# Pair 0 of an attention layer: the units of two heads issued in turns of two

## The chip, the cores and the metric

The kernel runs on one core of a Trainium2 chip. A core has a matrix engine (TensorE, PE in the profile, with its weight loads listed as PEld), three engines for elementwise work (VectorE or DVE, ScalarE or ACT, GpSimd or POOL), and a SyncE (SP) whose queue issues most DMA transfers. Each engine runs its own stream of instructions and waits for the others by semaphores. The metric is the device time of one execution in microseconds (us); the median of a few runs is given.

## The reference

The layer has 1024 positions and a width of 1024. The input is normalised and modulated, projected, mixed by 16 heads of 64, gated, projected again, added to the input and normalised. Eight heads do forgetting attention (a softmax). The other eight, with which the kernel begins, do stick-breaking attention:

```python
z = jnp.einsum('bhqd,bhkd->bhqk', q, k).astype(jnp.float32) * scale
strict = k_pos[None, :] < q_pos[:, None]
log_beta = jax.nn.log_sigmoid(z)
log_keep = jnp.where(strict, jax.nn.log_sigmoid(-z), 0.0)
later = lax.cumsum(log_keep, axis=3, reverse=True) - log_keep
w = jnp.where(strict, jnp.exp(log_beta + later), 0.0)
return jnp.einsum('bhqk,bhkd->bhqd', w.astype(v.dtype), v)
```

A query block of 128 rows sees only the keys up to its own end, so block i works on (i+1) x 128 keys.

## The kernel before

**Precision.** A matrix product in full precision is made of three (or two, with packed operands) products of fp32r parts: every operand is split into a rounded part ("hi") and the rest ("lo").

**Stages.** After a start phase (inputs, modulation, normalisation and transposition of x, and the projections of the first two pairs) comes the attention stage, from about 91 us on. The 16 heads form 8 pairs; pairs 0 to 3 are stick-breaking, pairs 4 to 7 forgetting attention. A *unit* (p, h, i) is query block i of head h of pair p; there are 16 to a pair, 128 in all.

**What a unit does** (stick-breaking):
- `att_query` (L383): ACT copies the unit's queries into one of two small buffers of its head (L388).
- `att_scores` (L397): PE writes the scores into the tile S (L410, L411). S has one buffer, two PSUM banks wide. ACT reads it twice, for the sigmoid of -z (L430, tile kp) and of z (L431, tile be). DVE makes the reverse running product of kp in one scan (L436), or two where there are more than 512 keys (L440), and POOL multiplies be by it (L444).
- `att_transpose` (L448): PE transposes the result 128 x 128 at a time into tiles T of up to four blocks (L461; two buffers). ACT casts each tile to its hi part (L463), DVE makes the lo part (L464), both called pt.
- `att_pv` (L469): once two neighbouring blocks 2j and 2j+1 of a head are transposed, PE multiplies them with v (L476), with 4j + 4 products, hi parts first. Block kb of v is needed by the product of key block kb; the last key block, 2j+1, comes after the first 2j hi products (or after one, for j = 0). ACT and DVE add up the result (L495, L496), POOL gates it (L497) and SP stores it (L505).

**Fillers.** Between these PE works on projections for later pairs, cut into steps by generators (`fillers`, L923). For pair 0 these are: one step with no PE work, the value tiles 4 to 7 of pairs 0 and 1 in two halves each (`v_tile`, L304: 12 matmuls at L310 to L312 per half, after the second half ACT copies the hi part, L318, and DVE subtracts, L319), with two small steps for the output gate beside them (L720), then one step that fetches weights, and eight weight steps of six matmuls (`m_step`, L251, lines L255 to L257). So tiles 0 to 3 of v are there when the stage begins, and tiles 4 to 7 come from the fillers.

**The order.** PE's order is written out by hand. The units stand in one list, `units`. The main loop (L969) goes over k: scores of unit k, queries of unit k+1, a fill, the product that has become ready, transposes of unit k-2 (`LAG`), another fill. How many filler steps have been done at each point comes from the list `want` (L956 to L963): pair p gets `FILL[p]` steps (18 for pair 0, some 36 for the others), shared out over its units by the weight `W0 + i + 1` with `W0` at 100, and `LEAD` looks ahead by two half places:

```python
fill(want[2 * k + LEAD + 1])
while ready:
    att_pv(*ready.pop(0))
...
fill(want[2 * k + LEAD + 2])
```

On ACT, DVE, POOL and SP the order isn't written by hand: it is worked out when the kernel is built, once and for the whole program, and each engine then runs its instructions in that fixed order.

The list itself comes from `order(p)` (L948): for pairs 0 to 3 head 0 with blocks 0 to 7, then head 1 with blocks 0 to 7; for pairs 4 to 6 each head downwards; for pair 7 two blocks of head 0 and two of head 1 in turns, downwards.

Of the kernel before, what the change touches and what calls it, by code (L numbers as in the profile page):

```python
# [16 lines left out]
NB = 8  # L17
# [10 lines left out]
def tile_hybrid_layer(  # L28
# [715 lines left out]
    for kb in range(NB):  # L744
# [13 lines left out]
        if kb < len(evacs):  # L758
            n, h = evacs[kb]
# [186 lines left out]
            next(fillers, None)  # L946

    def order(p):  # L948
        if p < 4:
            return [(p, h, i) for h in range(2) for i in range(NB)]  # L950
        if p < NPAIR - 1:
            return [(p, h, i) for h in range(2) for i in reversed(range(NB))]
        return [(p, h, i + d) for i in reversed(range(0, NB, 2)) for h in range(2) for d in (1, 0)]

    units = [u for p in range(NPAIR) for u in order(p)]
    want = [0.0]  # L956
    for p in range(NPAIR):
        size = [W0 + u[2] + 1 for u in order(p)]
        if p == NPAIR - 1:
            size = [1] * G7 + [0] * (16 - G7)  # L960
        for w in size:
            for _ in range(2):
                want.append(want[-1] + FILL[p] * w / (2 * sum(size)))  # L963
# [5 lines left out]
    for k in range(len(units) + LAG + 1):  # L969
        if k < len(units):  # L970
# [12 lines left out]
            p, h, i = units[k]  # L983
# [86 lines left out]
```

## Time and profile before

| | us |
|---|---|
| median of 3 runs | 689.89 |
| lowest, highest | 689.56, 691.04 |
| profiled execution | 689.48 |
| its span | 687.8 |
| mean granted TensorE clock in it | 0.997 |

The span is the time from the first to the last instruction in the trace. The profiled execution is one run by itself; its time stands beside the median to show how far the two agree. In rows of the timeline the first number is the start and the second the duration, both in us; then come the engine, the line of the kernel, the operation, the tile written and the tiles read, and how many instructions were merged into the row. A bracket names the idle time of the engine ahead of the row and the instruction that ended it.

### The profile page before, as it was taken

Reading aid. Unit: us, or ns where it says so; the run is one execution under the profiler, and the core shown is the slowest. Engines: PE = TensorE matmul, PEld = TensorE weight load, DVE = VectorE, ACT = ScalarE, POOL = GpSimd, SP = SyncE. Lnnn points to the kernel's source line nnn. Section 1 sums busy time; section 2 is a strip of 40 time slices with the busy share of each in tenths; the row PEclk is TensorE's granted clock in tenths of the full one; section 3 lists DMA queues with packets and bytes.
Section 4 is the critical chain, followed back from the end, with each engine's and each line's share of the span. In section 5 each row is a group of like instructions: output and inputs, shape, how many; then the busy total and the mean of one; then the engine's idle time right before and its main releaser. Section 6 shows DMA issues by size and latency. Waiting matters only on the chain.

```text
span 687.8 us, 11790 instructions
## 1 busy us (share of the span) xinstructions
PE 673.6 (98%) x4033; PEld 589.1 (86%) x4033; DVE 451.8 (66%) x924; ACT 381.9 (56%) x862; POOL 425.8 (62%) x555
## 2 busy tenths in 40 slices
PE   7999999999999999999999999999999999999996
PEld 4789898888998888889998888889988889888885
DVE  6895458767656676767675665656565767774645
ACT  4666457856557666666674564655565666531000
POOL 4567978656438565557388887877584364665411
PEclk9999999999999999999999999999999999999998
DMA  8966231011102122112134553444341298143301
GB/s 306 416 235 246 67 110 57 25 41 53 39 9 70 41 55 55 38 47 62 30 133 150 177 170 109 152 152 147 101 135 54 66 296 350 56 157 117 129 31 61
DMA packets 44316, 81.60 MB, mean 119 GB/s; under 512 B 5152, under 2 KB 18784, under 8 KB 43616
## 3 DMA queue, kind: packets, MB, share of 16 engines
q1 hardware_dynamic: 43104, 76.65, 34.1%
q10 hardware_dynamic: 1152, 4.19, 2.1%
q8 instruction: 32, 0.52, 0.3%
q14 instruction: 28, 0.23, 0.1%
HBM read 60.34 MB, written 16.29 MB: 111 GB/s over the span
## 4 chain that ended last, share of the span: by engine, by line
PE 93%; DVE 2%; DMA 1%; POOL 1%; SPq 1%; ACT 1%; issue 0%; POOLq 0%; DVEq 0%
PE m L255 10%; PE pv L476 10%; PE m L256 10%; PE m L257 10%; PE T L461 9%; PE S L411 5%; PE S L410 5%; PE o L853 4%; PE o L851 4%; PE o L852 4%; PE v L310 4%; PE v L311 4%; PE v L312 4%; DMA wss<-in_w_ss_dram 1%; PE st_q L573 1%; PE st_late L569 1%
## 5 line engine op out<-in xcount | busy, mean ns | idle before, releaser
L255 PE MATMUL m<-uh,whi 128*128 128x512 f32 x304 | 126.5, 416 | 0.5 <-DVE kl L243 0.5
L257 PE MATMUL m<-uh,wlo 128*128 128x512 f32 x304 | 119.7, 394 | 0.0
L256 PE MATMUL m<-ul,whi 128*128 128x512 f32 x304 | 119.7, 394 | 0.0
L464 DVE TENSOR_TENSOR pt<-T,pt 128x512 fp32r<-128x512 f32 (+2 forms) x192 | 100.6, 551 | 17.9 <-ACT pt L463 16.8
L444 POOL TENSOR_TENSOR be<-be,kp 128x127 f32<-128x127 f32 (+3 forms) x64 | 77.1, 1206 | 33.7 <-DVE kp L440 24.0
L463 ACT CAST pt<-T 128x512 fp32r<-128x512 f32 (+2 forms) x192 | 85.7, 480 | 16.8 <-PE T L461 13.0
L436 DVE TENSOR_TENSOR_SCAN kp<-kp,floor 128x512 f32<-128x512 f32 (+2 forms) x64 | 65.2, 1018 | 32.1 <-ACT kp L430 31.2
L476 PEld LDWEIGHTS pv<-pt,v 128*128 128x128 f32 (+1 forms) x640 | 77.1, 163 | 4.5 <-DVE pt L464 0.7
L476 PE MATMUL pv<-pt,v 128*128 128x256 f32 (+3 forms) x640 | 80.4, 271 | 0.5 <-DVE pt L464 0.5
L425 POOL TENSOR_SCALAR a<-a,l 128x1024 f32<-128x1024 f32 (+3 forms) x64 | 48.0, 749 | 39.6 <-DVE l L424 26.0
L257 PEld LDWEIGHTS m<-uh,wlo 128*128 128x128 f32 x304 | 57.1, 188 | 13.6
L423 ACT ACTIVATE a<-a,nm 128x1024 f32<-128x1024 f32 (+3 forms) x64 | 49.8, 778 | 34.1 <-DVE nm L417 33.0
L410 PE MATMUL S<-k,q 128*128 128x512 f32 (+5 forms) x192 | 66.5, 348 | 0.2 <-DVE nm L417 0.2
L411 PE MATMUL S<-kl,qz 128*128 128x512 f32 (+5 forms) x192 | 65.5, 342 | 0.0
L255 PEld LDWEIGHTS m<-uh,whi 128*128 128x128 f32 x304 | 57.3, 188 | 9.2 <-DVE kl L243 0.9
L256 PEld LDWEIGHTS m<-ul,whi 128*128 128x128 f32 x304 | 57.4, 189 | 8.0
L497 POOL TENSOR_TENSOR ty<-ty,sg 64x256 f32<-64x256 f32 x64 | 47.4, 741 | 25.0 <-DVE ty L496 12.8
L417 DVE CUSTOM_DVE_ANT_0 a<-S,fb 128x1024 f32<-128x1024 f32 (+3 forms) x64 | 48.3, 755 | 20.5 <-PE S L411 9.8
L430 ACT ACTIVATE kp<-S 128x128 f32<-128x128 f32 (+3 forms) x64 | 41.7, 651 | 31.8 <-PE S L411 29.7
L310 PE MATMUL v<-whi_v,uh 128*128 128x256 f32 (+1 forms) x192 | 56.1, 292 | 0.7 <-DVE kl L243 0.7
L388 ACT CAST qz<-q 64x128 fp32r<-64x128 f32 x128 | 37.4, 295 | 32.9 <-PE S L411 31.8
L311 PE MATMUL v<-whi_v,ul 128*128 128x256 f32 (+1 forms) x192 | 54.2, 282 | 0.0
(291 smaller groups left out, 1609.6 us busy)
## 6 DMA issues: line engine op xcount, KB each, us to landing
raw<-in_w_qkg_dram SPq DMA_DIRECT2D x38, 256.0 KB, 3.0
wss<-in_w_ss_dram SPq DMA_DIRECT2D x5, 1024.0 KB, 9.0
x<-in_x_dram SPq DMA_DIRECT2D x8, 512.0 KB, 7.6
k<-k SPq DMA_DIRECT2D x32, 128.0 KB, 2.4
wg<-in_w_gate_dram SPq DMA_DIRECT2D x8, 512.0 KB, 4.5
raw_o<-in_w_out_dram SPq DMA_DIRECT2D x16, 256.0 KB, 2.7
fb<-f_dr ACTq DMA_DIRECT2D x8, 512.0 KB, 4.2
wo_dr<-whi_o SPq DMA_DIRECT2D x16, 256.0 KB, 2.7
```

Source lines behind the costliest of these rows:

```text
L255: nc.tensor.matmul(acc, hi[:, c], u_hi[kt][:, s], start=(kt == 0), stop=False)
L256: nc.tensor.matmul(acc, hi[:, c], u_lo[kt][:, s], start=False, stop=False)
L257: nc.tensor.matmul(acc, lo[:, c], u_hi[kt][:, s], start=False, stop=(kt == NB - 1))
L310: nc.tensor.matmul(acc[:, :n], u_hi[kt][:, ts_], hi[:, s], start=(kt == 0), stop=False)
L311: nc.tensor.matmul(acc[:, :n], u_lo[kt][:, ts_], hi[:, s], start=False, stop=False)
L410: nc.tensor.matmul(S[:, s, :w], qst[p][h][:, qs], kst[p][h][:, ks], start=True, stop=False)
L411: nc.tensor.matmul(S[:, s, :w], z, klo[p][:, ks], start=False, stop=True)
L436: scan = nc.vector.tensor_tensor_scan(rv, rv, floor[0][:, 512 - n:][:, ::-1], initial=0.0, op0=ALU.mult, op1=ALU.max)
L444: nc.gpsimd.tensor_tensor(be[:, :ke - 1], be[:, :ke - 1], kp[:, 1:ke], op=ALU.mult)
L463: nc.scalar.copy(hi[:, :n, qo:qo + P], t3)
L464: nc.vector.tensor_tensor(lo[:, :n, qo:qo + P], t3, hi.bitcast(F32)[:, :n, qo:qo + P], op=ALU.subtract)
L476: nc.tensor.matmul(acc[:m, q0:256], vt[p][:, kb, h * P:h * P + m], pt[:, kb % 4, q0:], start=start, stop=stop)
```

## The change

For pair 0 alone `order` returns another list. Head 0 still goes upwards by pairs of blocks, head 1 goes downwards by pairs of blocks (each pair of blocks upwards in itself), and the two take turns, two units at a time.

```diff
     def order(p):
+        if p == 0:
+            return [(p, h, (6 - i if h else i) + d) for i in range(0, NB, 2) for h in range(2) for d in (0, 1)]
         if p < 4:
             return [(p, h, i) for h in range(2) for i in range(NB)]
```

The list of pair 0, as (head, block): before (0,0) (0,1) (0,2) (0,3) (0,4) (0,5) (0,6) (0,7) (1,0) (1,1) (1,2) (1,3) (1,4) (1,5) (1,6) (1,7); after (0,0) (0,1) (1,6) (1,7) (0,2) (0,3) (1,4) (1,5) (0,4) (0,5) (1,2) (1,3) (0,6) (0,7) (1,0) (1,1). The products of two neighbouring blocks come at the same loop steps, k = 4, 6, 8 and so on to 18, but in the order of the new list. Since `want` is weighted by the block number, some filler steps move by one place. All the work, its instructions and its sizes are the same.

## The prediction

> **What bounds the kernel now.** I read the page first, for its busy shares and its chain of work that ended last.
>
> ```profile
> span 687.8 us, 11790 instructions
> PE 673.6 (98%) x4033; PEld 589.1 (86%) x4033; DVE 451.8 (66%) x924; ACT 381.9 (56%) x862; POOL 425.8 (62%) x555
> PE 93%; DVE 2%; DMA 1%; POOL 1%; SPq 1%; ACT 1%; issue 0%; POOLq 0%; DVEq 0%
> ```
>
> TensorE (PE) is busy for 673.6 of 687.8 us and makes 93% of the chain. The change adds and removes no instruction. It can only move the time by making PE wait less, or more, while pair 0's units are in work. So the question is how much PE waits there now. The windows view over that stretch comes next (start:end, length, busy time of PE, PEld, DVE, ACT and POOL, then the granted clock).
>
> ```profile
> 91.00:111.00 20.00, 20.00 (x153) 18.96 (x151) 15.10 (x27) 14.40 (x39) 13.38 (x22) 1.00 0.32 83
> 111.00:131.00 20.00, 18.68 (x117) 16.46 (x116) 14.81 (x25) 14.33 (x33) 13.35 (x20) 1.00 0.13 38
> 131.00:172.00 41.00, 40.86 (x233) 35.13 (x232) 30.17 (x45) 27.25 (x59) 26.06 (x35) 1.00 0.18 48
> ```
>
> PE is short of full only by 1.32 us in the middle window and 0.14 in the last. DVE, ACT and POOL are at 64 to 76%, so none is the bound on average. What counts is who is late at single points. The waits of PE between 84 and 200 us name three:
>
> ```profile
> PE T L461 <- DVE pt L464: 0.8, 1, 0.8
> PE v L310 <- DVE kl L243: 0.7, 1, 0.7
> PE pv L476 <- DVE pt L464: 0.5, 1, 0.5
> ```
>
> The second lies at pair 1's end and the change does not touch it. The timeline of PE shows the other two, and a third that the waits leave out.
>
> ```profile
> 110.61 0.39 PE L410 MATMUL S<-k,q 128*128 128x512 f32 x1
> 110.84 0.39 PE L411 MATMUL S<-kl,qz 128*128 128x512 f32 x1
> 112.02 0.85 PE L461 MATMUL T<-ident,be 128*128 128x128 f32 x6 [0.79 <-DVE pt L464]
> 112.63 0.48 PE L255 MATMUL m<-uh,whi 128*128 128x512 f32 x1
> 114.11 0.22 PE L410 MATMUL S<-k,q 128*128 128x128 f32 x1
> 114.28 0.75 PE L476 MATMUL pv<-pt,v 128*128 128x256 f32 x5
> 115.55 0.98 PE L476 MATMUL pv<-pt,v 128*64 128x256 f32 x7 [0.53 <-DVE pt L464]
> ...
> 137.72 0.40 PE L257 MATMUL m<-uh,wlo 128*128 128x512 f32 x1
> 138.26 0.84 PE L461 MATMUL T<-ident,be 128*128 128x128 f32 x6
> ...
> 103.15 0.58 PE L476 MATMUL pv<-pt,v 128*128 128x256 f32 x4
> 103.57 0.49 PE L461 MATMUL T<-ident,be 128*128 128x128 f32 x3
> ```
>
> I take the loss from start to start. A 512-column matmul is followed 0.23 us later by the next (110.61 to 110.84), so the scores of the widest unit were through at 111.07, and the transposes start at 112.02: 0.95 us lost. Four products take 0.42 us (103.15 to 103.57), 0.105 each. The five at 114.28 were through at 114.81, and the next starts at 115.55: 0.74 lost. The last weight matmul at 137.72 was through at 137.95, and the transposes start at 138.26: 0.31 lost. Together **2.00 us**: this is all that a better order of pair 0 can win.
>
> The bracketed idle times (0.79 and 0.53) give 1.32. The Trainium skill, Perfetto Trace Analysis, section "Tensor Engine Instruction (MATMUL, LD_WEIGHTS)", says that a matmul's start is recorded, while its end is computed from its size. By the ends the removable loss would be 1.32 us and my sum below would come out at +0.76 instead of +0.08. The trace sides with the starts: the matmul at 110.61 "lasts" 0.39 us but is followed after 0.23.
>
> **The change, part by part.** The loop step k issues: scores of unit k, a fill, the head product that is ready, transposes of unit k-2, a fill. Working through the weights in `want`, the fills fall as before but for these. At k=3 the first half of v tile 6 moves ahead of the transposes. At k=6 and 7 a weight fetch moves one slot (no PE work in it). At k=11 a weight step moves ahead of the transposes. At k=14 another fetch comes one slot earlier. Products stay at every even k, so the y stores keep their places in SP's queue, and weight loads behind them too. The counts on POOL, ACT and DVE are the same.
>
> New is which unit sits at which k: widths (in blocks of 128 keys) 1, 2, **7, 8**, 3, 4, 5, 6, 5, 6, 3, 4, **7, 8**, 1, 2. The old waits, at k=7, 8 and 15, hit a 6-block unit and a product with widths of 5 to 8 in a row around them; I remove all three, -2.00. What is late next?
>
> *The score buffer.* There is one, so the scores of unit k+1 wait until ACT has read those of unit k twice (L430, L431).
>
> ```profile
> 107.35 0.28 PE L310 MATMUL v<-whi_v_2b,uh 128*128 128x256 f32 x1
> 108.37 0.91 ACT L431 ACTIVATE be<-S 128x896 f32<-128x896 f32 x1
> 112.19 1.02 ACT L431 ACTIVATE be<-S 128x1024 f32<-128x1024 f32 x1
> ...
> 98.33 0.73 PE L720 MATMUL gate<-gate,half 128*128 128x512 f32 x2
> 98.90 0.39 PE L410 MATMUL S<-k,q 128*128 128x512 f32 x1
> 99.46 0.41 PE L461 MATMUL T<-ident,be 128*128 128x128 f32 x2
> 99.63 0.36 PE L310 MATMUL v<-v_home,uh 128*128 128x256 f32 x1
> 101.74 0.28 PE L310 MATMUL v<-whi_v_2b,uh 128*128 128x256 f32 x1
> ...
> 106.03 0.60 PE L461 MATMUL T<-ident,be 128*128 128x128 f32 x4
> 106.43 0.47 PE L410 MATMUL S<-k,q 128*128 128x448 f32 x1
> ```
>
> A 1024-wide unit holds the buffer from 111.07 to 113.21 (112.19 + 1.02): 2.14 us. An 896-wide one holds it from 107.35 to 109.28 (108.37 + 0.91): 1.93. PE's own work must cover that. Its pieces: half a v tile 1.41 (101.74 to 103.15), a gate step 0.57 (98.33 to 98.90), a weight step 1.48 (112.63 to 114.11), two transposes 0.17 (99.46 to 99.63), four 0.40 (106.03 to 106.43).
> - k=2 to 3 (896): half a v tile and a gate step, 1.98, against 1.93: nothing.
> - k=3 to 4 (1024): half a v tile and two transposes, 1.58, against 2.14: **0.56 lost**.
> - k=7 to 8 (768, so at most 1.93): a weight step and four transposes, 1.88: at most 0.05, taken as nothing.
> - k=13 to 14 (1024): the same 1.88 against 2.14: **0.26 lost**.
> - Elsewhere a product or a narrow unit leaves a margin. Behind each wait the whole of PE's queue stands, so it counts in full.
>
> *The last v tile.* Head 1's last product now comes at k=6, right behind the second half of v tile 7 (the ninth fill), which it reads; before it came at k=18. It can do six products (0.63) before it needs that tile.
>
> ```profile
> 99.23 0.28 DVE L319 TENSOR_TENSOR v<-v,v 128x128 fp32r<-128x128 f32 x1
> 108.77 0.99 PE L476 MATMUL pv<-pt,v 128*128 128x256 f32 x8
> 109.35 0.26 ACT L318 CAST v<-v 128x128 fp32r<-128x128 f32 x1
> 110.69 0.27 DVE L319 TENSOR_TENSOR v<-v,v 128x128 fp32r<-128x128 f32 x1
> ```
>
> Tile 5 was through on PE at 98.33 and in SBUF at 99.51: 1.18 us, a wait of 0.55. Tile 7 took from 108.77 to 110.96, 2.19, a wait of 1.56, because ACT and DVE were in a wide unit. The copy and subtraction alone (0.26 + 0.27) would fit under 0.63, so the ends are 0 and 1.56. Ahead of tile 5 the unit in work was 384 wide, ahead of tile 7 it was 896; in the new order it is 640, half way between: I take **1.05**.
>
> *Products behind a fresh transpose.* At k=8, 10 and 14 a product follows closely, as the one that lost 0.74 at 114.81.
>
> ```profile
> 106.96 0.75 DVE L440 TENSOR_TENSOR_SCAN kp<-kp,floor 128x256 f32<-128x256 f32 x1
> 113.64 1.28 DVE L440 TENSOR_TENSOR_SCAN kp<-kp,floor 128x512 f32<-128x512 f32 x1
> 115.44 1.99 POOL L444 TENSOR_TENSOR be<-be,kp 128x1023 f32<-128x1023 f32 x1
> ```
>
> There the unit in DVE's way was 1024 wide; at k=10 it is 768, whose second scan is 0.53 shorter (1.28 less 0.75): 0.74 - 0.53 = **0.21** at k=10. At k=8 the transposes are four, not six, and at k=14 a weight step lies in between: nothing, with 0.74 as the upper end for each of the three.
>
> *Long chain of the early wide unit.* Its weights were ready 6.36 us after its scores were through (115.44 + 1.99, less 111.07), with POOL crowded. At k=3 PE has until its transposes three half tiles (4.23), transposes of two and at least six (0.17 and 0.61), a product (0.42), a 512-wide score (98.90 to 99.46, 0.56), a narrower one (at least 0.17) and the 0.56 of waiting: 6.72. Covered, by 0.36; if not, it costs the difference.
>
> **The sum.** -2.00 + 0.56 + 0.26 + 1.05 + 0.21 = **+0.08 us**. The profiled execution took 689.48 us, 1.68 of them outside the span; the median of the three runs is 689.89, 0.41 above it. Added to the median: 690.0 us. A measurement of this kernel can tell 0.2%, 1.38 us, from no change. With the last-tile and product waits at their lower ends (0) the sum is -1.18 (688.7), with them at their upper ends (1.56 and three times 0.74) it is +2.60 (692.5).
>
> **The rivals.** *Slower: the score buffer sets the pace, because casts get ahead of sigmoids.* The v copy at 109.35 stood behind the 896-wide sigmoid that ended at 109.28, though its tile was through at 108.77; it can go the other way round. If two v copies (0.26 each) stand ahead of the sigmoids at k=2 and 3, and two transposed-tile casts at k=7 and 13, each place loses that on top.
>
> ```profile
> 106.66 0.58 ACT L463 CAST pt<-T 128x512 fp32r<-128x512 f32 x1
> ```
>
> Two places by 0.52 and two by 1.16 make 3.36, so 693.4; half of it 691.7; the middle 692.5. It decides from 1.30 us on (1.38 less 0.08), some three casts. For it: the k=2 and k=7 covers have no margin (0.05 either way). Against: before 111.27, ACT finished its small work while PE was still writing scores. Chance 0.30.
>
> *Faster: the old waits go and the new ones don't come.* With the last tile and the products at 0, -1.18; if the 0.7 us at pair 1's end (the kl row) also goes, because DVE's order is worked out anew from pair 0 on, -1.9: 688.0. For it: the narrow units after the wide ones give ACT and DVE room. Against: pair 1's code is the same, and two score waits stand on plain durations. Chance 0.13.
>
> *Sum as forecast, a shift of waits, not of time:* 690.0, chance 0.57, its own range 688.6 to 691.3.
>
> **How the numbers follow.** The time is that of the sum, 690.0. The range goes down to 688.3, between the sum's low end and the faster rival's 688.0, and up to 692.8, past the sum's high end and the middle of the slower rival. The chances are the cases': faster 0.13, within 0.2% 0.57, slower 0.30.
>
> **What would show it.** Right: the two bracketed waits at 112.02 and 115.55 and the 0.31 at 138 are gone; in their place a gap of about 0.6 us ahead of the fifth unit's scores (near 103 us) with the second sigmoid as its end; a gap of about 1 us inside the first 16-product block (near 111 us), ended by DVE L319; 0.3 us ahead of the 15th unit's scores; PE idle between 91 and 150 us of much the same size as now; the granted clock still 1.00. Wrong: a gap of over 1 us ahead of scores at k=3, 4, 8 or 14, with casts on ACT ahead of the sigmoids (the slower rival); transposes of the early wide units waiting for POOL L444 (the chain was not covered); no gap at the 16-product block (the tile was out in time); or waits that come or go after 180 us, which no step here explains.

## The result, and the profile after

The changed kernel takes 692.12 us in the median (691.62 to 693.27, 6 runs), the kernel before 689.67 (6 runs): a ratio of 1.0036, with a 95% interval of 1.0025 to 1.0046. It is slower by about 2.45 us. The prediction had 690.0 within 688.3 to 692.8, gave "within 0.2%" a chance of 0.57 and "slower" 0.30. The time lies inside the range, but the case that came is "slower", not the one held likeliest.

The page of the profile after, its first lines:

```profile
span 690.0 us, 11795 instructions
PE 675.2 (98%) x4033; PEld 589.8 (85%) x4033; DVE 452.2 (66%) x924; ACT 382.4 (55%) x862; POOL 427.0 (62%) x555
```

The span has grown by 2.2 us, PE's busy time by only 1.6 (and a busy PE can hide waiting, as the start-to-start reading showed), and the counts of the five engines are the same. The waits of PE between 84 and 200 us, as they were shown for before:

```profile
PE pv L476 <- DVE pt L464: 0.9, 2, 0.5
PE v L310 <- DVE kl L243: 0.7, 1, 0.7
PE pv L476 <- DVE v L319: 0.7, 1, 0.7
PE S L410 <- ACT be L431: 0.6, 2, 0.4
```

The transposes wait no more; products and scores do. The second line is the same wait at pair 1's end as before. It serves as a mark: where does the row after it start, in the kernel before and in the changed one?

```profile
176.43 0.39 PE L310 MATMUL v<-whi_v,uh 128*128 128x264 f32 x1 [0.74 <-DVE kl L243]
```

```profile
178.70 0.39 PE L310 MATMUL v<-whi_v,uh 128*128 128x264 f32 x1 [0.74 <-DVE kl L243]
```

The first scores of pair 0 start at 91.24 and at 91.30. From there to the mark it is 85.19 us before and 87.40 after: **2.21 us more, which is the whole growth of the span**. I call this length the stage; it leaves out the start phase, which differs by up to 0.6 us from one profile to the next. PE's timeline of the changed kernel shows where the time is lost:

```profile
101.77 0.38 PE L461 MATMUL T<-ident,be 128*128 128x128 f32 x2
102.59 0.44 PE L410 MATMUL S<-k,q 128*128 128x384 f32 x1 [0.44 <-ACT be L431]
...
110.60 0.88 PE L476 MATMUL pv<-pt,v 128*128 128x256 f32 x6
112.15 1.33 PE L476 MATMUL pv<-pt,v 128*128 128x128 f32 x10 [0.68 <-DVE v L319]
113.32 0.49 PE L461 MATMUL T<-ident,be 128*128 128x128 f32 x3
...
114.36 0.60 PE L461 MATMUL T<-ident,be 128*128 128x128 f32 x4
...
116.67 0.30 PE L411 MATMUL S<-kl,qz 128*128 128x320 f32 x1
117.05 0.56 PE L476 MATMUL pv<-pt,v 128*128 128x256 f32 x3
118.04 0.75 PE L476 MATMUL pv<-pt,v 128*64 128x256 f32 x5 [0.42 <-DVE pt L464]
118.62 0.71 PE L461 MATMUL T<-ident,be 128*128 128x128 f32 x5
...
121.28 0.82 PE L461 MATMUL T<-ident,be 128*128 128x128 f32 x6
...
123.50 0.34 PE L411 MATMUL S<-kl,qz 128*128 128x384 f32 x1
123.78 0.80 PE L476 MATMUL pv<-pt,v 128*128 128x256 f32 x5
125.04 0.99 PE L476 MATMUL pv<-pt,v 128*64 128x256 f32 x7 [0.47 <-DVE pt L464]
125.88 0.71 PE L461 MATMUL T<-ident,be 128*128 128x128 f32 x5
...
136.50 0.60 PE L461 MATMUL T<-ident,be 128*128 128x128 f32 x4
137.29 0.33 PE L410 MATMUL S<-k,q 128*128 128x128 f32 x1 [0.20 <-ACT be L431]
139.00 1.35 PE L476 MATMUL pv<-pt,v 128*128 128x256 f32 x8
140.19 0.93 PE L461 MATMUL T<-ident,be 128*128 128x128 f32 x7
```

Read from start to start, as in the prediction. The lengths of products that don't wait are taken from two experiments below, where they are shown: 16 products 1.80 us, 12 products 1.32, 8 products 0.83 (rows of the kernel before that don't wait give 1.78, 1.32 and 0.82). The scores at 116.67 (320 columns) and 123.50 (384) were through 0.15 and 0.17 us after their start, so the places below begin at 116.82 and 123.67.

| place | forecast | measured | how |
|---|---|---|---|
| old waits, gone | -2.00 | -2.00 | both bracketed rows and the 0.31 are gone; a new wait at k=8 is counted below |
| scores at k=4 | 0.56 | 0.65 | 101.77 + 0.17 to 102.59 |
| last v tile, k=6 | 1.05 | 0.92 | 110.60 to 113.32, less 1.80 |
| product at k=8 | 0 | 0.97 | 116.82 to 118.62, less 0.83 |
| product at k=10 | 0.21 | 0.89 | 123.67 to 125.88, less 1.32 |
| scores at k=14 | 0.26 | 0.39 | 136.50 + 0.40 to 137.29 |
| product at k=14 | 0 | 0.36 | 139.00 to 140.19, less 0.83 |
| sum | +0.08 | +2.18 | stage: +2.21 |

Every wait is where it was looked for. One kind of them, the products, is 2.22 instead of 0.21.

### The profile page after: what moved, and what is told of

It reads as the page before. It is cut to its first block, busy times and chain, and to the rows that moved or that the text cites. A ratio compares the mean times of both kernels' runs of the same rounds, so it can differ in the third digit from the quotient of the medians.

```text
span 690.0 us, 11795 instructions
## 1 busy us (share of the span) xinstructions
PE 675.2 (98%) x4033; PEld 589.8 (85%) x4033; DVE 452.2 (66%) x924; ACT 382.4 (55%) x862; POOL 427.0 (62%) x555
## 4 chain that ended last, share of the span: by engine, by line
PE 87%; DMA 5%; DVE 3%; POOL 2%; issue 1%; ACT 1%; POOLq 0%; SPq 0%; DVEq 0%; ACTq 0%
PE pv L476 10%; PE m L255 9%; PE m L256 9%; PE m L257 9%; PE T L461 8%; PE S L411 5%; PE S L410 5%; PE o L853 4%; PE o L851 4%; PE o L852 4%; PE v L310 4%; PE v L311 4%; PE v L312 4%; DMA wss<-in_w_ss_dram 3%; DMA raw<-in_w_qkg_dram 1%
## 5 line engine op out<-in xcount | busy, mean ns | idle before, releaser
L464 DVE TENSOR_TENSOR pt<-T,pt 128x512 fp32r<-128x512 f32 (+3 forms) x192 | 100.7, 552 | 18.8 <-ACT pt L463 17.6
L444 POOL TENSOR_TENSOR be<-be,kp 128x127 f32<-128x127 f32 (+3 forms) x64 | 77.2, 1206 | 36.4 <-DVE kp L440 26.5
L463 ACT CAST pt<-T 128x512 fp32r<-128x512 f32 (+3 forms) x192 | 85.8, 481 | 17.6 <-PE T L461 14.2
L476 PE MATMUL pv<-pt,v 128*64 128x256 f32 (+3 forms) x640 | 81.4, 272 | 1.8 <-DVE pt L464 0.9
```

The costliest lines, as they stand in the source:

```text
L444: nc.gpsimd.tensor_tensor(be[:, :ke - 1], be[:, :ke - 1], kp[:, 1:ke], op=ALU.mult)
L463: nc.scalar.copy(hi[:, :n, qo:qo + P], t3)
L464: nc.vector.tensor_tensor(lo[:, :n, qo:qo + P], t3, hi.bitcast(F32)[:, :n, qo:qo + P], op=ALU.subtract)
L476: nc.tensor.matmul(acc[:m, q0:256], vt[p][:, kb, h * P:h * P + m], pt[:, kb % 4, q0:], start=start, stop=stop)
```

## The experiments

The theory after this reading: each of these waits is a cost by itself, caused by too little PE work between the scores of a wide unit and the product or transposes behind them, and goes when PE gets other work there. The rival: ACT and DVE are behind in this stretch as a whole, so that a wait taken away at one place comes back at the next. All ratios are to the kernel before, run beside it on the same chip (its medians were 689.61, 689.66 and 689.76 us).

**1. The v tile one slot earlier.**

```diff
-        fill(want[2 * k + LEAD + 2])
+        fill(want[2 * k + LEAD + 2] + (k == 5))
```

> The changed kernel with one filler step moved: the second half of v tile 7 comes at the end of k=5, one slot earlier, so that scores and transposes lie between it and the 16-product block that reads it. Theory (each of the waits seen in the changed kernel's trace is a cost by itself): the 0.94 us lost inside that block goes, ratio to before about 1.0023 (691.3 us) instead of 1.0036. Rival (the wait is only the place where a general lateness of ACT and DVE shows): the loss moves to the next scores or product and the time stays at 692.1, ratio 1.0036.

Measured: 691.21 us, ratio 1.0025 (1.0016 to 1.0033). The stage is 86.47 us, 0.93 shorter than in the changed kernel. Its 16-product block, in PE's timeline:

```profile
110.84 1.97 PE L476 MATMUL pv<-pt,v 128*128 128x256 f32 x16
112.64 0.49 PE L461 MATMUL T<-ident,be 128*128 128x128 f32 x3
```

Sixteen products in one piece, 1.80 us. Nothing came up in its place, and the time is what the theory expected. The theory holds for this wait.

**2. Fills ahead of the product.**

```diff
+        if ready and k < 15:
+            fill(want[2 * k + LEAD + 2])
         while ready:
             att_pv(*ready.pop(0))
```

> The changed kernel with, in pair 0, the second fill of a step issued ahead of the product instead of behind the transposes; this puts one weight step (1.4 us of PE work) ahead of the products at k=8 and k=10, and leaves the count of all work alone. Theory (products come on PE before their lo parts are out, 0.90 and 0.85 us at these two places): both waits go, 690.4 us, ratio 1.0010. Rival (ACT and DVE are full, so that the wait reappears ahead of the next transposes, whose tile buffers are not free): 691.5 to 692.1, ratio 1.003 or more.

Measured: 691.06 us, ratio 1.0022 (1.0014 to 1.0031); stage 86.37, 1.03 shorter, where 1.75 was expected. PE's timeline at k=8, 9 and 10:

```profile
118.37 0.99 PE L476 MATMUL pv<-pt,v 128*128 128x256 f32 x8
119.20 0.71 PE L461 MATMUL T<-ident,be 128*128 128x128 f32 x5
...
121.36 0.84 PE L461 MATMUL T<-ident,be 128*128 128x128 f32 x6 [0.75 <-DVE pt L464]
...
125.15 1.48 PE L476 MATMUL pv<-pt,v 128*128 128x256 f32 x12
126.47 0.71 PE L461 MATMUL T<-ident,be 128*128 128x128 f32 x5
```

The product at k=8 runs without a wait (118.37 to 119.20, 0.83 us), and so does the one at k=10 (1.32 us). But the weight step that now stands ahead of the product no longer stands between the transposes of k=8 and those of k=9, and these wait for the two tile buffers to be emptied: the same kind of wait as at 112.02 in the kernel before. The rival is right here in part: one weight step can't cover both places.

**3. Both of these, with the fills first at every step.**

```diff
+        if 7 <= k < 15:
+            fill(want[2 * k + LEAD + 2])
         while ready:
             att_pv(*ready.pop(0))
...
-        fill(want[2 * k + LEAD + 2])
+        fill(want[2 * k + LEAD + 2] + (k == 5))
```

> The changed kernel with the v tile half one slot earlier and, from k=7 to k=14, both fills of a step ahead of the product and the transposes (so that no transposes stand close behind others without a weight step between, where the second run had its new wait of 0.9 us). If the waits seen are separate costs, 0.93 us (v) and 1.75 us (two products) go, and the two score waits (0.65, 0.39) stay: 2.45 - 2.68 = -0.2 us against before, ratio 0.9997. If a wait of 0.7 to 0.9 us comes up again elsewhere because DVE is full in this stretch: ratio 1.0008 to 1.0012.

Measured: 689.66 us, ratio 0.9997 (0.9988 to 1.0006); stage 84.47. With a weight step ahead of every product and every set of transposes, none of them is named in PE's waits any more; the two score waits are left:

```profile
PE S L410 <- ACT be L431: 0.6, 2, 0.4
```

So the new order is level with the kernel before once the filler steps suit it (the stage is 0.7 us shorter than before, which the interval of the ratio takes in). The rival is out for these three waits: they did not move on to another place before the mark.

**4. Without the second scan, in both orders.**

```diff
-            if ke > n:
+            if ke > n and p > 0:
```

In the changed kernel:

> The changed kernel without the second scan (L440, keys further back than 512) in pair 0; it leaves out that part of the running product for the units of 640 keys and more, 0.48 to 1.28 us of DVE time each. If it is DVE's scans that hold up the lo parts of the products, the product waits at k=8 and k=10 fall from 0.90 and 0.85 to 0.3 or less each and the v wait shrinks too: 690.6 us, ratio 1.0015. If it is ACT, whose casts stand behind the two sigmoids of the unit just scored, the lo parts come at most 0.3 us earlier at each place: 691.5 us, ratio 1.0028.

Measured: 690.13 us, ratio 1.0007 (0.9998 to 1.0016); stage 85.48, 1.92 shorter.

```profile
111.91 1.32 PE L476 MATMUL pv<-pt,v 128*128 128x128 f32 x10 [0.17 <-DVE v L319]
...
116.80 0.56 PE L476 MATMUL pv<-pt,v 128*128 128x256 f32 x3
117.53 0.75 PE L476 MATMUL pv<-pt,v 128*64 128x256 f32 x5 [0.16 <-DVE pt L464]
...
123.18 1.71 PE L476 MATMUL pv<-pt,v 128*128 128x256 f32 x12
...
137.86 1.00 PE L476 MATMUL pv<-pt,v 128*128 128x256 f32 x8
```

The brackets shrink (0.16 instead of 0.42 at k=8, 0.17 instead of 0.68 at the v tile, none at k=10). Counted by starts, as in the table, the loss falls from 0.89 to 0.26 us at k=10 and from 0.92 to 0.40 at the v tile, and the 0.36 at k=14 is gone (the row behind 137.86 starts at 138.70, 0.84 later). At k=8 it falls only from 0.97 to 0.71. So DVE's scans stand in the way of the lo parts at k=10 and k=14, as the first theory of this run said. At k=8 the rest is ACT's, as the second said: in this run DVE has no second scan there and waits for the cast, which ACT starts at 116.16, behind the two sigmoids of the unit just scored.

```profile
116.78 0.69 DVE L464 TENSOR_TENSOR pt<-T,pt 128x512 fp32r<-128x512 f32 x1 [0.36 <-ACT pt L463]
```

In the kernel before:

> The kernel before without the second scan (L440) in pair 0, the same part left out as in the changed kernel's run of this kind (the running product beyond the nearest 512 keys). The changed kernel lost 1.9 us by it. If DVE's scans are what the waits of both kernels hang on, the kernel before loses its waits too (0.95, 0.74 and 0.31): ratio 0.9975, and the two kernels without the scan lie 2.2 us apart as the full ones do. If the scans matter only in the new order, ratio 0.9993 to 1.0000.

Measured: 688.24 us, ratio 0.9979 (0.9970 to 0.9988); stage 83.73, 1.46 shorter. The product's wait is gone. The transposes at k=7 still wait, in PE's timeline of this run:

```profile
111.64 0.84 PE L461 MATMUL T<-ident,be 128*128 128x128 f32 x6 [0.58 <-DVE pt L464]
```

This wait hangs on ACT and DVE together (DVE's subtraction waits 0.17 us for ACT's cast there), not on the scans alone. So the stage gains 1.46 of the 2.00 us; the interval of the ratio takes in the 0.9975 that was expected. The two kernels without the scan are 1.9 us apart, the full ones 2.45.

**5. The turns alone, both heads upwards.**

```diff
-            return [(p, h, (6 - i if h else i) + d) for i in range(0, NB, 2) for h in range(2) for d in (0, 1)]
+            return [(p, h, i + d) for i in range(0, NB, 2) for h in range(2) for d in (0, 1)]
```

> The turns without the downward run: both heads of pair 0 upwards, two units at a time (widths 1 2 1 2 3 4 3 4 5 6 5 6 7 8 7 8). If the cost of the change is in its wide units among the v tiles at the beginning (scores wait 0.65, v wait 0.94), this order has none of it: 690.1 us or less, ratio at most 1.0010. If the cost is in taking turns itself (products of two heads close behind units of the other head), it stays at 691 to 692, ratio 1.002 to 1.0036; three products behind 5 to 8 block units, 0.8 us each, and no wait at v or at the early scores would make 690.4, ratio 1.0010, in between.

Measured: 690.13 us, ratio 1.0007 (0.9998 to 1.0015), not to be told from before; stage 85.27, 0.08 longer than before.

```profile
PE S L410 <- ACT be L431: 0.9, 1, 0.9
PE pv L476 <- DVE pt L464: 0.8, 1, 0.8
```

The v wait and the early score wait are gone. PE's waits name one score wait (at k=8, where no fill came between) and one product wait (k=10), about 1 us each when counted by starts.

**6. The downward run alone, no turns.**

```diff
-            return [(p, h, (6 - i if h else i) + d) for i in range(0, NB, 2) for h in range(2) for d in (0, 1)]
+            return [(p, h, (6 - i if h else i) + d) for h in range(2) for i in range(0, NB, 2) for d in (0, 1)]
```

> The downward run without the turns: head 0 with blocks 0 to 7, then head 1 by pairs of blocks downwards (widths 1 to 8, then 7 8 5 6 3 4 1 2). The v tiles are all out when head 1 begins, and no wide unit stands among them. If the early place of the wide units is what the downward run costs, nothing of it is left here; the waits of before at k=7 and 8 (0.95, 0.74) stay, and the products behind the second 7 and 8 block units may wait 0.7 us once more: ratio 1.0000 to 1.0012. If the downward run costs wherever it stands, 1.0025 or more.

Measured: 688.85 us, ratio 0.9986 (0.9977 to 0.9995): faster than expected; stage 84.08, 1.11 shorter than before. PE's timeline from k=7 on:

```profile
111.77 0.85 PE L461 MATMUL T<-ident,be 128*128 128x128 f32 x6 [0.77 <-DVE pt L464]
112.38 0.47 PE L255 MATMUL m<-uh,whi 128*128 128x512 f32 x1
113.85 0.37 PE L410 MATMUL S<-k,q 128*128 128x448 f32 x1
114.67 1.64 PE L476 MATMUL pv<-pt,v 128*128 128x256 f32 x12
```

The first eight units are those of before, with the same wait at k=7. But the scores of k=8 are now 896 keys wide and take PE 0.82 us (113.85 to 114.67) instead of 0.17, and the product behind them runs almost in one piece (1.47 us, a wait of 0.15), where before it waited 0.74. I had left this cover out of the expectation. Together with the 0.31 at k=15, which is gone too, that makes 0.9 of the 1.1; the rest was not traced. So neither part of the change costs 2.2 us by itself: head 1 downwards gains 1.1 when it stands alone, the turns cost nothing that can be measured, and the two together put the 7 and 8 block units among the v tiles. That accounts for the early score wait and the v wait, 1.57 us together, which neither run 5 nor run 6 has; the product waits stand behind 6 and 8 block units, and run 5 has one of that kind too.

**7. Fills first with three other orders.** First the plain turns of run 5, with one weight step earlier at k=7 and the fills first from k=10:

```diff
+        if 10 <= k < 15:
+            fill(want[2 * k + LEAD + 2])
         while ready:
             att_pv(*ready.pop(0))
...
-        fill(want[2 * k + LEAD + 2])
+        fill(want[2 * k + LEAD + 2] + (k == 7))
```

> Turns with both heads upwards, and two moves of filler steps worked out from that run's trace: one weight step earlier at k=7 (ahead of the scores that waited 1.0 us) and, from k=10 to 14, both fills ahead of product and transposes (the product at k=10 waited 0.96 us). If waits go where PE has a weight step to cover them: 1.7 us less than the plain turns, ratio 0.998 to before. If the waits only move: ratio 1.0000 to 1.0007.

Then the kernel before with the fills first from k=7:

```diff
+        if 7 <= k < 15:
+            fill(want[2 * k + LEAD + 2])
         while ready:
             att_pv(*ready.pop(0))
```

> The kernel before, its order of units untouched, with both fills of a step ahead of the product and the transposes from k=7 to k=14. If the waits of before (transposes at k=7 0.95, product at k=8 0.74) come from too little PE work ahead of them, not from the order of the units, both go: 1.7 us less, ratio 0.9976. If DVE and ACT are simply behind in that stretch, the wait moves on: ratio 0.9990 to 1.0000.

And the same lines in the downward run of run 6:

> The downward run without turns, and both fills of a step ahead of product and transposes from k=7 to k=14. The downward run alone has one wait left in pair 0 (0.93 us ahead of the transposes at k=7). If a weight step ahead covers it, no wait is left: 1.1 + 0.9 = 2.0 us less than before, ratio 0.9971, no better than the kernel before with the same fills (0.9975) by more than 0.3 us. If the fill takes the cover from a product instead: 0.998 or more.

Measured: 688.31 us, ratio 0.9978 (0.9970 to 0.9987); 688.06 us, 0.9975 (0.9965 to 0.9986); 687.64 us, 0.9970 (0.9960 to 0.9981). The stages are 83.55, 83.45 and 83.22. All three beat both kernels, and each ratio is close to what was expected if waits go where PE has work to cover them (0.998, 0.9976, 0.9971). The windows view, 91 to 150 us (PE's busy time is the third number), for the changed kernel and then for the last of these three:

```profile
91.00:150.00 59.00, 56.58 (x373) 50.19 (x372) 43.05 (x69) 40.18 (x94) 38.21 (x55) 1.00 0.20 53
```

```profile
91.00:150.00 59.00, 59.00 (x393) 53.42 (x392) 44.93 (x73) 42.59 (x101) 39.59 (x58) 1.00 0.20 54
```

In the second, PE shows no idle time at all, and 20 matmul records more in the same 59 us. Among these three, the order of the units matters little: from the first to the last it is 0.33 us of stage, and their intervals overlap, so that none is shown to be the best. The changed order is the exception. With its fills first (run 3) it has a stage of 84.47, 1.02 us longer than the kernel before with its fills first, and 689.66 us against 688.06, with intervals that don't overlap. The two score waits that run 3 keeps (0.65 and 0.40 by starts) are of that size.

## Why the prediction was off in size

**Right: what bounds the stage, and what the change can win.** The 2.00 us of old waits went, read from start to start; by the brackets the balance would not close (1.3 before, 2.2 after, 0.9 more, against 2.21). The three fill-first runs, with stages 1.64 to 1.97 us shorter than before, come near that 2.00 but not over it.

**Right: the score buffer, the last v tile, the early wide units.** 0.56 and 0.26 against 0.65 and 0.39; 1.05 against 0.92, and run 1 shows that it is a cost by itself. The 1.05 was the middle of two cases that differed by 1 us, so that it came this near is in part luck. The chain of the early wide unit was covered: no transposes wait for POOL L444.

**Wrong: the term "products behind a fresh transpose".** It had 0.21 us, at k=10 alone, and measures 2.22. The step that failed is this: I took the 0.74 us of the kernel before and shortened it by the 0.53 that DVE's scan is shorter. What runs ahead of the product starts at the end of the scores, not at the transposes: the two sigmoids of the unit just scored, then the cast, on ACT; its scans, then the lo part, on DVE. In the changed kernel, ACT's timeline ahead of the product at k=8, and then DVE's:

```profile
114.56 0.81 ACT L430 ACTIVATE kp<-S 128x768 f32<-128x768 f32 x1 [0.16 <-PE S L411]
115.26 0.81 ACT L431 ACTIVATE be<-S 128x768 f32<-128x768 f32 x1
116.09 0.30 ACT L388 CAST qz<-q 64x128 fp32r<-64x128 f32 x1
116.42 0.59 ACT L463 CAST pt<-T 128x512 fp32r<-128x512 f32 x1
```

```profile
115.40 1.22 DVE L436 TENSOR_TENSOR_SCAN kp<-kp,floor 128x512 f32<-128x512 f32 x1 [0.42 <-ACT kp L430]
116.66 0.75 DVE L440 TENSOR_TENSOR_SCAN kp<-kp,floor 128x256 f32<-128x256 f32 x1
117.32 0.67 DVE L464 TENSOR_TENSOR pt<-T,pt 128x512 fp32r<-128x512 f32 x1
```

The transposed tile was through on PE at about 114.71 (the next matmul starts there), but its cast starts at 116.42 and its lo part is out at 117.99. From the end of the scores to the lo products it is 3.68 us (114.36 to 118.04), and PE had four transposes, a weight step, the next scores and three hi products: 0.35 + 1.48 + 0.63 + 0.32 = 2.78. That gives 0.90 of the 0.97. At k=10 the same sum is 3.76 (121.28 to 125.04) against 0.57 + 1.48 + 0.34 + 0.53 = 2.92: 0.84 of the 0.89.

And the kernel before? There it was 4.48 us (111.07 to 115.55), against 0.61 + 1.48 + 0.17 + 0.53 = 2.79 of work. The difference is 1.69, not 0.74, because PE stood 0.95 us at the transposes first, and in that time ACT and DVE got ahead. The wait at the transposes was cover for the product. I took it off in full and kept the product's short wait as the measure. With sums of this kind the two products behind 768-wide units are 1.74 us instead of 0.21, and the whole +1.6 instead of +0.08: a slower kernel, where the forecast said no change. These lengths are read from the changed kernel, but the kernel before had the chain too, behind its own 768-wide unit at k=5, where PE had enough work to cover it:

```profile
104.60 0.28 PE L310 MATMUL v<-v_home,uh 128*128 128x256 f32 x1
107.62 0.67 DVE L464 TENSOR_TENSOR pt<-T,pt 128x512 fp32r<-128x512 f32 x1
```

The scores were through at 104.60 and the lo part was out at 108.29: 3.69 us. PE's work takes 0.40 + 1.48 + 0.59 + 0.32 of it at k=8 and 0.61 + 1.48 + 0.35 + 0.53 at k=10 (transposes, a weight step, scores and hi products, all as they run in the kernel before), which leaves 0.90 and 0.72. So the forecast could have been made without the new trace. The third product, at k=14, was put at nothing because a weight step lies ahead of it; it measures 0.36. Its lo part runs on DVE from 138.88 to 139.55, right behind the second scan of a 1024-wide unit, and without that scan (run 4) the wait is gone.

That the stated range holds the result is luck in this respect: its upper end had the three products at 0.74 each, 2.22 together, which is the measured total, made of other parts.

**The rivals.** "Slower" came true, at 692.12, near the 692.5 given for it, but not by its mechanism: no casts stood ahead of the sigmoids at the wide units (the first sigmoid starts 0.20 to 0.25 us after the last scores were through at k=2, 3, 7 and 13; at k=7 it is the row at 114.56 above, with scores through at 114.36), and run 3 takes the two large product waits away and leaves the score waits as they were. "Waits only shift" was the idea behind the likeliest case; the balance came out 2.1 us to the other side.

**Not settled:** no kernel was tried that removes the two score waits (0.65 and 0.39) of the changed order. Nor was another order on ACT and DVE tried, with the cast ahead of the second sigmoid or the lo part ahead of the second scan; whether the chain itself could be shortened without making the scores wait stays open.

## What to carry to other kernels

When a wait disappears, its time was cover for whatever waits next: work out each new wait from the moment the chain behind it starts (here the end of the scores), with all that PE does in between, and not by scaling the wait that is left over. On a full engine that issues in a fixed order, put independent work ahead of the step that needs a fresh result, at every step, before trying other orders: that one change of place gave 1.6 us, more than either reordering. Two changes that are harmless alone, turns and direction, can be costly together: here the wide units came among the v tiles only with both (1.57 of the 4.18 us of new waits). Try them one at a time.

## What the runs showed of the hardware

In this case a matmul's start is the thing to count by: 16 products in a row took 0.11 us each from start to start, though one such product lasts 0.27 us on the mean of the page, and the losses counted by starts (2.18) close with the stage (2.21), while the brackets in the waits of the changed kernel add up to 0.9 + 0.7 + 0.6 = 2.2 and those of before to 1.3, a difference of 0.9. The granted clock reads 1.00 between 91 and 150 us in every run: waits of about 1 us and less did not lower it there.
